# Half of the weights' low parts made by adding transfers instead of VectorE and GpSimd

## The chip, the cores and the metric

The kernel runs on one core of a Trainium2 chip. The metric is the device time of one execution in microseconds (us); the time of the kernel before is the median of three runs. The engines are named as in the profile: PE (TensorE, matrix products), PEld (its weight loads), DVE (VectorE), ACT (ScalarE), POOL (GpSimd) and SP (SyncE, which here only issues transfers). A transfer is a DMA; "SPq" is SP's own instruction stream.

## The reference

One layer of a decoder trunk on 288 positions (256 of a prompt, and 8 sequences of 4 new tokens), in float32. The width is 2048.

```
h = rmsnorm(x); proj = h @ w_in + b_in              # 2048 -> 3072: a, gate, z of 1024 each
u = a * sigmoid(gate)
c = silu(layernorm(depthwise_conv31(history + u)))  # 31 taps for each channel
d = moving_mean(history + z, windows 2, 4, 8, 16) - z
p = (d @ pool_w, per group of 256 channels) * pool_scale
x = x + concat(c, p) @ w_out                        # 2048 -> 2048
x = x + square(relu(rmsnorm(x) @ w_ff1)) @ w_ff2    # 2048 -> 8192 -> 2048
y = rmsnorm(x)
```

Outputs are y and the new histories of u and z.

## The kernel before, in words

Channels lie on the 128 partitions and the 288 positions along the free axis. Weights come from memory in blocks of 128 x 8 x 256 numbers (1 MB), one `wr` tile each, through a pool of three such tiles (`wraw`). SP issues these loads in a fixed order.

To multiply in float32 precision with products of the type float32r, each weight block is split into two parts: `hi`, the weight rounded to float32r, and `lo`, the weight minus `hi`. The function `split` does that for the two **halves** of a block (4 slices of 128 x 256, thus 128 x 1024 numbers): ACT casts the half into a `whi` tile, and another engine subtracts it from the raw weight into a `wlo` tile. `whi` and `wlo` come from pools of **four tiles each** (`wspl`), so the split of a half can start only when PE has finished the half that used the tile before. `gemm` then issues three products for every slice and each of two column blocks: hi x hi (line 250), hi x lo of the activations (line 251), lo x hi (line 252). A half is thus 24 products of 128 x 128 by 128 x 288.

Which engine subtracts is decided by a running count with the table `SHARE`: out of eight halves, so many go to POOL (in two pieces of 128 x 512), the others to DVE.

```
SHARE = {"first": 0, "second": 4, "conv": 7, "pool": 5, "pool_w": 3, "w_out": 6}
...
            turn["n"] += share
            slow = turn["n"] >= 8
            turn["n"] %= 8
```

The stages, in the order in which PE passes them:

- Input projection, 12 groups of four halves (96 products each): seven convolution groups, four pooling groups (window 16 first, then 8, 4, 2), and the last convolution group. Each group's result is a pair of PSUM banks `ac`; there are two such pairs. A convolution group is followed by its gate (`conv_pair`): a product with the row `rb` on DVE (`ag`), a sigmoid on ACT, two DVE operations into `u_all`, then 30 taps of 128 x 256 on DVE (line 340, tile `pc`) and, for the 32 sample positions, four products on POOL (line 343, `prd`). The taps have low priority and fill DVE whenever nothing else is ready. A pooling group (`pool_group`) goes DVE (`tz`), ACT (into `z_all`), POOL (line 369, one pair of sums `s` for each doubling of the window), DVE (`d`), ACT and DVE (`dx`, the hi and lo of the activations).
- `pool_w`: four small products groups of 12 on `dx`, whose weights are one block. ACT and DVE bring each result out of its banks as `px` (lines 417 and 418).
- Output projection `w_out`: 16 groups of two halves. The first eight, with the `px` activations, are split by the table; from the ninth on DVE subtracts everything.
- The two feed-forward products in four chunks, with all subtractions on DVE, and the last norm.

Every engine takes its instructions in the order in which they were put into its stream. That order comes out of the tile framework's scheduler, which runs the program with estimated durations and picks by priority; it is fixed when the kernel is built. An instruction that waits holds up everything behind it on its engine.

Halves are numbered here as in the names of the tiles: `whi9`/`wlo9` belong to the first half of the third group, 29 to 32 to the first pooling group, 45 to 48 to the last convolution group, 49 and 50 to `pool_w`, 51 to 66 to the first eight groups of the output projection.

Of the kernel before, what the change touches and what calls it, by code (L numbers as in the profile page):

```python
# [17 lines left out]
D = 2048  # L18
# [48 lines left out]

SHARE = {"first": 0, "second": 4, "conv": 7, "pool": 5, "pool_w": 3, "w_out": 6}

# [11 lines left out]
def trunk_kernel(ctx: ExitStack, tc: tile.TileContext, io):  # L81
# [43 lines left out]
    def f32(t):  # L125
        return t.bitcast(F32)
# [19 lines left out]
    def load(cuts=((0, 8),), x_cuts=()):  # L146

        raw = wraw.tile([P, 8, 256], F32, name=nm("wr"), tag="wr")
        src = io["w"][next(blocks)]
        for j, (k0, k1) in enumerate(cuts):  # L150
            if j < len(x_cuts):
                a, b = x_cuts[j]
                nc.sync.dma_start(xT[:, a:b, :], io["xT"][:, a:b, :])
            nc.sync.dma_start(raw[:, k0:k1, :], src[:, k0:k1, :])
        return raw

# [53 lines left out]

    turn = {"n": 0}

    def split(raw, share=0, cut=4):


        parts = []
        for h in range(2):
            hi = wspl.tile([P, 4, 256], F32R, name=nm("whi"), tag="whi")
            lo = wspl.tile([P, 4, 256], F32R, name=nm("wlo"), tag="wlo")
            turn["n"] += share  # L220
            slow = turn["n"] >= 8
            turn["n"] %= 8
            for k in range(0, 4, cut):
                src = raw[:, 4 * h + k : 4 * h + k + cut, :]
                nc.scalar.copy(hi[:, k : k + cut, :], src)  # L225
                eng, step = (nc.gpsimd, 2) if slow else (nc.vector, cut)
                for j in range(k, k + cut, step):
                    eng.tensor_tensor(lo[:, j : j + step, :], raw[:, 4 * h + j : 4 * h + j + step, :], hi[:, j : j + step, :].bitcast(F32), op=ALU.subtract)  # L228
            parts.append((hi, lo))
# [46 lines left out]
    def weight_groups():  # L276

        yield [split(raw0, SHARE["first"], 2), split(raw1, SHARE["first"], 2)]
        for j, (kind, _) in enumerate(SEQUENCE[1:]):
            yield [split(load(), SHARE[kind if j else "second"]) for _ in range(2)]  # L280
        getp = split(load(), SHARE["pool_w"])
        for g in GROUPS:
            yield [lambda k, m, g=g: getp(2 * g + k, m)]
        for _ in range(8):
            get = split(load(), SHARE["w_out"])
            yield [lambda k, m, get=get: get(korder[k], m)]
# [304 lines left out]
```

## Time and profile before

| | |
|---|---|
| median of three runs | 1122.64 us (1118.34 to 1123.49) |
| the profiled execution | 1121.02 us, of which its span (first to last instruction) 1119.2 us |
| PE busy | 1095.0 us, 98% of the span |
| PEld / DVE / ACT / POOL busy | 1090.7 / 646.2 / 470.1 / 185.8 us |
| mean granted TensorE clock | 0.990 |
| bytes moved | 187.0 MB, 167 GB/s |

How to read it: a group of instructions is given by line, engine, operation and tiles, with its count, its total busy time, the mean duration of one in ns, and the idle time of the engine just ahead of it with what ended that. Products are pipelined: each shows about 0.3 us, but they start some 0.13 us apart, so the number of products that start in a stretch tells more than PE's busy time. A stretch of the span gets one row with each engine's busy time and number of instructions, the granted TensorE clock, the busy share of the 16 DMA engines and the rate.

### The profile page before, as it was taken

The page shows a single profiled execution, that of the slowest core. Times are in us where ns is not written, and L with a number is a line of the kernel's source. Part 1 is how long each engine was busy: PE and PEld are TensorE (multiplying, and loading weights), DVE is VectorE, ACT ScalarE, POOL GpSimd, SP SyncE. Part 2 cuts the span into 40 slices and gives each one's busy share as a digit, 9 for nine tenths or more (in the row PEclk, how much of TensorE's full clock was granted, in tenths as well). Part 3 has the DMA queues.
Part 4 walks back from the last instruction along what each step waited for, and adds up shares of the span by engine and source line. Part 5 has one row for each costly group of instructions (what it writes and reads, how often), then busy time and mean ns, then how long its engine had stood idle before and what let it go on. Part 6 is the DMA issues. An engine that isn't in the chain of part 4 may idle for free.

```text
span 1119.2 us, 19178 instructions
## 1 busy us (share of the span) xinstructions
PE 1095.0 (98%) x8220; PEld 1090.7 (97%) x8220; DVE 646.2 (58%) x830; ACT 470.1 (42%) x578; POOL 185.8 (17%) x185
## 2 busy tenths in 40 slices
PE   9999988999999999999999999999999999999995
PEld 8999987999999999999999999999999999999995
DVE  7799999667654444444554444455444445554553
ACT  8444444465444433334443333444433334444441
POOL 1898996512100000000000000000000000000000
PEclk9999998999999999999999999999999999999997
DMA  9545456444444454544445444454544545445432
GB/s 344 186 154 185 151 132 201 154 176 161 160 168 162 161 179 153 179 159 164 175 154 182 153 168 171 155 184 152 172 167 160 180 151 177 162 159 180 152 112 85
DMA packets 31909, 187.00 MB, mean 167 GB/s; under 512 B 3408, under 2 KB 7760, under 8 KB 10448
## 3 DMA queue, kind: packets, MB, share of 16 engines
q1 hardware_dynamic: 31680, 185.73, 48.1%
q8 instruction: 64, 1.05, 0.4%
q14 instruction: 21, 0.17, 0.0%
q10 hardware_dynamic: 144, 0.05, 0.0%
HBM read 181.49 MB, written 4.28 MB: 166 GB/s over the span
## 4 chain that ended last, share of the span: by engine, by line
PE 93%; POOL 2%; DVE 2%; DMA 1%; ACT 1%; issue 1%; SPq 0%; DVEq 0%; ACTq 0%; POOLq 0%
PE ac L250 31%; PE ac L252 31%; PE ac L251 30%; POOL wlo L228 1%; POOL s L369 1%; DMA wr<-in_w 1%; PE pt L186 0%; DMA xT<-in_xT 0%; DVE xT L531 0%; ACT whi L225 0%; ACT hx L271 0%; PE pr L204 0%; DVE px L418 0%; DVE hx L272 0%; DVE pc L340 0%
## 5 line engine op out<-in xcount | busy, mean ns | idle before, releaser
L225 ACT CAST whi<-wr 128x1024 fp32r<-128x1024 f32 (+1 forms) x342 | 355.2, 1040 | 563.6 <-PE ac L251 531.9
L228 DVE TENSOR_TENSOR wlo<-wr,whi 128x1024 fp32r<-128x1024 f32 (+1 forms) x297 | 364.0, 1226 | 352.2 <-ACT whi L225 351.3
L250 PE MATMUL ac<-ax,whi 128*128 128x288 f32 x1024 | 303.4, 296 | 0.0
L250 PE MATMUL ac<-fx,whi 128*128 128x288 f32 x1024 | 303.1, 296 | 0.0
L252 PE MATMUL ac<-ax,wlo 128*128 128x288 f32 x1024 | 301.8, 295 | 0.0
L252 PE MATMUL ac<-fx,wlo 128*128 128x288 f32 x1024 | 301.8, 295 | 0.0
L251 PE MATMUL ac<-ax,whi 128*128 128x288 f32 x1024 | 298.5, 292 | 0.0
L251 PE MATMUL ac<-fx,whi 128*128 128x288 f32 x1024 | 298.5, 292 | 0.0
L251 PEld LDWEIGHTS ac<-ax,whi 128*128 128x128 f32 x1024 | 192.5, 188 | 0.1
L251 PEld LDWEIGHTS ac<-fx,whi 128*128 128x128 f32 x1024 | 192.5, 188 | 0.0
L250 PEld LDWEIGHTS ac<-ax,whi 128*128 128x128 f32 x1024 | 192.4, 188 | 0.1
L250 PEld LDWEIGHTS ac<-fx,whi 128*128 128x128 f32 x1024 | 192.4, 188 | 0.0
L252 PEld LDWEIGHTS ac<-ax,wlo 128*128 128x128 f32 x1024 | 191.5, 187 | 0.0
L252 PEld LDWEIGHTS ac<-fx,wlo 128*128 128x128 f32 x1024 | 191.5, 187 | 0.0
L228 POOL TENSOR_TENSOR wlo<-wr,whi 128x512 fp32r<-128x512 f32 x90 | 119.4, 1358 | 48.1 <-ACT whi L225 48.1
L252 PE MATMUL ac<-hx,wlo 128*128 128x288 f32 x384 | 114.8, 299 | 1.5 <-DVE wlo L228 1.3
L250 PE MATMUL ac<-hx,whi 128*128 128x288 f32 x384 | 114.8, 299 | 0.3 <-ACT whi L225 0.3
L251 PE MATMUL ac<-hx,whi 128*128 128x288 f32 x384 | 112.7, 294 | 0.0
L340 DVE SCALAR_TENSOR_TENSOR pc<-u_all,vec,pc 128x256 f32<-128x256 f32 x232 | 99.4, 480 | 1.2
L252 PEld LDWEIGHTS ac<-hx,wlo 128*128 128x128 f32 x384 | 72.6, 189 | 3.4 <-DVE wlo L228 2.5
L250 PEld LDWEIGHTS ac<-hx,whi 128*128 128x128 f32 x384 | 72.9, 190 | 0.6 <-ACT whi L225 0.5
L251 PEld LDWEIGHTS ac<-hx,whi 128*128 128x128 f32 x384 | 72.9, 190 | 0.1
(109 smaller groups left out, 828.4 us busy)
## 6 DMA issues: line engine op xcount, KB each, us to landing
wr<-in_w SPq DMA_DIRECT2D x167, 1024.0 KB, 4.9
xT<-in_xT SPq DMA_DIRECT2D x8, 288.0 KB, 5.7
wr<-in_w SPq DMA_DIRECT2D x8, 256.0 KB, 5.6
out_u_out<-u_all SPq DMA_DIRECT2D x1, 1208.0 KB, 8.9
out_yT<-xT SPq DMA_DIRECT2D x2, 576.0 KB, 2.9
u_all<-in_hist_c SPq DMA_DIRECT2D x8, 136.0 KB, 6.1
out_z_out<-z_all SPq DMA_DIRECT2D x1, 668.0 KB, 8.1
z_all<-in_hist_p SPq DMA_DIRECT2D x4, 152.0 KB, 5.6
```

The costliest lines, as they stand in the source:

```text
L225: nc.scalar.copy(hi[:, k : k + cut, :], src)
L228: eng.tensor_tensor(lo[:, j : j + step, :], raw[:, 4 * h + j : 4 * h + j + step, :], hi[:, j : j + step, :].bitcast(F32), op=ALU.subtract)
L250: nc.tensor.matmul(b, wh, xh, start=k == 0, stop=False)
L251: nc.tensor.matmul(b, wh, xl, start=False, stop=False)
L252: nc.tensor.matmul(b, wl, xh, start=False, stop=k == n - 1)
L340: nc.vector.scalar_tensor_tensor(out=dst, in0=up[:, w : w + SEQ], scalar=cwv[:, w : w + 1], in1=pc, op0=ALU.mult, op1=ALU.add)
L369: nc.gpsimd.tensor_tensor(s2[:, m, 2 * w - 1 :], s[:, m, 2 * w - 1 :], s[:, m, w - 1 : ZL - w], op=ALU.add)
```

## The change

The table of shares is replaced by a table of ways for each half of a group: "V" subtracts on DVE, "G" on POOL, and "D" is new. For a D half ACT first casts the weight into `hi` as before, then writes -`hi` into the `lo` tile, and then POOL issues a transfer that fetches the same half of the weight block a second time from memory and adds it to what is in the `lo` tile (`accum_op=ALU.add`). `load` returns the source beside the tile for that. With the first D half three small DVE operations take the difference between the subtraction and the transfer's result for one slice and add it, times 2^20, to the activations' last tile, so a difference would be seen in the output.

```diff
-SHARE = {"first": 0, "second": 4, "conv": 7, "pool": 5, "pool_w": 3, "w_out": 6}
+WAYS = {"first": ("VV", "VV"), "second": ("VG", "VG"), "conv": ("DG", "DG"), "pool": ("DG", "DV"), "pool_w": ("DV",), "w_out": ("DG",)}
...
-        return raw
+        return raw, src
...
-    def split(raw, share=0, cut=4):
+    def split(raw, ways="VV", cut=4):
+        raw, src = raw
         parts = []
-        for h in range(2):
+        for h, way in enumerate(ways):
             hi = wspl.tile([P, 4, 256], F32R, name=nm("whi"), tag="whi")
             lo = wspl.tile([P, 4, 256], F32R, name=nm("wlo"), tag="wlo")
-            turn["n"] += share
-            slow = turn["n"] >= 8
-            turn["n"] %= 8
             for k in range(0, 4, cut):
...
+                if way == "D":
+                    continue
+                eng, step = (nc.gpsimd, 2) if way == "G" else (nc.vector, cut)
...
+            if way == "D":
+                nc.scalar.activation(lo, f32(hi), AF.Copy, scale=-1.0)
+                if not proof:
+                    proof.append(tmp("q")[:, 0:256])
+                    nc.vector.tensor_tensor(proof[0], raw[:, 4 * h, :], f32(hi[:, 0, :]), op=ALU.subtract)
+                nc.gpsimd.dma_start(lo, src[:, 4 * h : 4 * h + 4, :], accum_op=ALU.add)
...
-            yield [split(load(), SHARE[kind if j else "second"]) for _ in range(2)]
-        getp = split(load(), SHARE["pool_w"])
+            yield [split(load(), ways) for ways in WAYS[kind if j else "second"]]
+        getp = split(load(), *WAYS["pool_w"])
```

Of the 62 halves from the second group to the eighth group of the output projection, POOL subtracted 45 and DVE 17; now POOL subtracts 26, DVE 7, and 29 are D halves. The feed-forward products are split as before.

The scheduler's order moves with it. First, ACT in a convolution group (the casts of halves 17 to 20; `ag` is the gate of the group before). Before:

```order
L225 CAST whi17_857<-wr9_855 128x1024
L225 CAST whi18_861<-wr9_855 128x1024
L225 CAST whi19_868<-wr10_866 128x1024
L225 CAST whi20_873<-wr10_866 128x1024
L326 ACTIVATE ag4_878<-ag4_878,vec_85 128x288
```

Now:

```order
L226 CAST whi17_862<-wr9_860 128x1024
L233 ACTIVATE wlo17_863<-whi17_862 128x1024
L226 CAST whi18_867<-wr9_860 128x1024
L226 CAST whi19_874<-wr10_872 128x1024
L233 ACTIVATE wlo19_875<-whi19_874 128x1024
L226 CAST whi20_879<-wr10_872 128x1024
L339 ACTIVATE ag4_884<-ag4_884,vec_85 128x288
```

Two negations of 128 x 1024 have come in per group, each right behind its cast.

Second, POOL from the end of the convolution groups into the first pooling group (`prd` are a convolution group's sample products, `s` the pooling sums, `sum_c` a sum over convolution results). Before:

```order
L343 TENSOR_TENSOR prd7_1417<-u_all_87,vec_85 128x8x31 x4
L228 TENSOR_TENSOR wlo34_1529<-wr17_1522,whi34_1528 128x512 x2
L349 TENSOR_TENSOR sum_c_213<-c1_506,c2_717 128x288
L228 TENSOR_TENSOR wlo36_1540<-wr18_1533,whi36_1539 128x512 x2
L369 TENSOR_TENSOR s1_1550<-z_all_88 128x422 x2
L228 TENSOR_TENSOR wlo37_1673<-wr19_1670,whi37_1672 128x512 x2
L369 TENSOR_TENSOR s2_1553<-s1_1550 128x420 x2
L228 TENSOR_TENSOR wlo39_1684<-wr20_1681,whi39_1683 128x512 x2
L369 TENSOR_TENSOR s3_1556<-s2_1553 128x416 x2
L228 TENSOR_TENSOR wlo40_1689<-wr20_1681,whi40_1688 128x512 x2
L369 TENSOR_TENSOR s4_1559<-s3_1556 128x408 x2
```

Now:

```order
L356 TENSOR_TENSOR prd7_1424<-u_all_87,vec_85 128x8x31 x4
L237 DMA wlo33_1532<-in_w 128x1024
L231 TENSOR_TENSOR wlo34_1537<-wr17_1529,whi34_1536 128x512 x2
L237 DMA wlo35_1544<-in_w 128x1024
L382 TENSOR_TENSOR s1_1558<-z_all_88 128x422 x2
L382 TENSOR_TENSOR s2_1561<-s1_1558 128x420 x2
L237 DMA wlo37_1681<-in_w 128x1024
L382 TENSOR_TENSOR s3_1564<-s2_1561 128x416 x2
L231 TENSOR_TENSOR wlo38_1686<-wr19_1678,whi38_1685 128x512 x2
L382 TENSOR_TENSOR s4_1567<-s3_1564 128x408 x2
L237 DMA wlo39_1693<-in_w 128x1024
```

The issues of the adding transfers stand in POOL's stream among the sums and the subtractions, each behind what is written above it.

Third, ACT around `pool_w` (the sigmoid `ag8` and the table load belong to the last convolution group; `px1` to `px4` bring out the four results). Before:

```order
L417 ACTIVATE px1_2171<-ac13_2158,vec_85 128x288 x2
L225 CAST whi52_2232<-wr26_2225 128x1024
L326 ACTIVATE ag8_2109<-ag8_2109,vec_85 128x288
L384 CAST dx4_1998<-d4_1991 128x2x288
L168 ACT_TABLE_LOAD
L168 ACTIVATE few_111<-ag8_2109 128x1
L225 CAST whi53_2370<-wr27_2368 128x1024
L417 ACTIVATE px2_2189<-ac14_2176,vec_85 128x288
L337 ACTIVATE pc8_2115<-u_all_87,vec_85 128x256
L417 ACTIVATE px3_2207<-ac15_2194,vec_85 128x288
L417 ACTIVATE px2_2189<-ac14_2176,vec_85 128x288
```

Now:

```order
L339 ACTIVATE ag8_2119<-ag8_2119,vec_85 128x288
L168 ACT_TABLE_LOAD
L168 ACTIVATE few_111<-ag8_2119 128x1
L430 ACTIVATE px1_2181<-ac13_2168,vec_85 128x288
L350 ACTIVATE pc8_2125<-u_all_87,vec_85 128x256
L430 ACTIVATE px1_2181<-ac13_2168,vec_85 128x288
L226 CAST whi53_2380<-wr27_2378 128x1024
L430 ACTIVATE px2_2199<-ac14_2186,vec_85 128x288
L233 ACTIVATE wlo53_2381<-whi53_2380 128x1024
L430 ACTIVATE px2_2199<-ac14_2186,vec_85 128x288
L430 ACTIVATE px3_2217<-ac15_2204,vec_85 128x288
```

All `px` now stand behind the sigmoid and the table load: on PE the first `pool_w` products (those that make `px1`) used to stand inside the last convolution group, 22 products ahead of its end, and now all four groups of them follow it.

More of the change, by code (lines that the diff above doesn't have):

```diff
@@ L276, in weight_groups @@
     def weight_groups():
[L278 removed]
+        yield [split(raw, ways, 2) for raw, ways in zip((raw0, raw1), WAYS["first"])]
         for j, (kind, _) in enumerate(SEQUENCE[1:]):
[L280 to L281 removed]
+            yield [split(load(), ways) for ways in WAYS[kind if j else "second"]]
+        getp = split(load(), *WAYS["pool_w"])
         for g in GROUPS:
@@ L284, in weight_groups @@
         for _ in range(8):
-            get = split(load(), SHARE["w_out"])
+            get = split(load(), *WAYS["w_out"])
             yield [lambda k, m, get=get: get(korder[k], m)]
```

12 lines of the change are left out of this document (7 added, 5 removed).

## The prediction

> **What bounds the kernel now.** I read the page's head first: PE is busy 98% of the span, so the change can win only what PE loses now, and can lose wherever it makes PE wait. The table by stretches of the span shows where PE loses; the count behind PE's busy time is of products begun.
>
> ```profile
> span 1119.2 us, 19178 instructions
> PE 1095.0 (98%) x8220; PEld 1090.7 (97%) x8220; DVE 646.2 (58%) x830; ACT 470.1 (42%) x578; POOL 185.8 (17%) x185
> ...
> core 0: us, PE busy (x) PEld busy (x) DVE busy (x) ACT busy (x) POOL busy (x), PEclk, DMA share, GB/s
> ...
> 140.00:154.00 14.00, 14.00 (x108) 14.00 (x107) 13.96 (x28) 5.56 (x10) 14.00 (x14) 1.00 0.44 152
> 154.00:168.00 14.00, 10.09 (x66) 9.29 (x65) 13.65 (x23) 5.79 (x9) 14.00 (x11) 0.92 0.58 116
> 168.00:182.00 14.00, 9.11 (x51) 8.66 (x50) 13.02 (x30) 9.36 (x15) 10.12 (x10) 0.83 0.64 223
> 182.00:196.00 14.00, 13.66 (x90) 13.56 (x91) 12.81 (x26) 4.73 (x8) 7.16 (x7) 0.88 0.64 175
> 196.00:210.00 14.00, 14.00 (x107) 13.89 (x106) 7.71 (x14) 5.18 (x6) 9.20 (x9) 1.00 0.46 153
> ...
> 400.00:700.00 300.00, 300.00 (x2271) 300.00 (x2270) 140.25 (x127) 109.87 (x111) 0.00 (x0) 1.00 0.48 165
> ```
>
> A full stretch of 14 us holds 107 or 108 products (300 us hold 2271, so one per 0.132 us). From 154 to 196 us there are 66 + 51 + 90 = 207 instead of some 322: 115 x 0.132 = 15.2 us lost, of which PE is idle for 3.91 + 4.89 + 0.34 = 9.1 us; most of the rest is the clock (0.92, 0.83, 0.88). These are the end of the input projection and `pool_w`. Taking off about 0.7 us that the products for the mean need there, **14.5 us** can be won; before and after it, in the stages that the change touches, PE waits for nothing. The waits themselves, by time:
>
> ```profile
> start us, us, engine line op out<-in xcount [idle before <-releaser]
> ...
> 166.42 0.61 PE L252 MATMUL ac<-dx,wlo 128*128 128x288 f32 x1 [3.75 <-DVE wlo L228]
> 166.83 0.44 PE L250 MATMUL ac<-dx,whi 128*128 128x288 f32 x1
> 167.07 0.44 PE L251 MATMUL ac<-dx,whi 128*128 128x288 f32 x1
> ...
> 174.96 0.40 PE L250 MATMUL ac<-dx,whi 128*128 128x288 f32 x1 [1.26 <-DVE px L418]
> ...
> 182.34 0.40 PE L250 MATMUL ac<-dx,whi 128*128 128x288 f32 x1 [3.97 <-DVE px L418]
> ```
>
> One wait is for a `lo` part that DVE made late, two for banks (`px`). After the first, products start 0.24 us apart (166.83, 167.07): an idle stretch of this length costs clock as well. In the stretch ahead DVE (13.96 of 14) and POOL (14.00) are both full: subtractions, taps and pooling sums are late together.
>
> **The change part by part.** The prices of what is moved:
>
> ```profile
> L228 DVE TENSOR_TENSOR wlo<-wr,whi 128x1024 fp32r<-128x1024 f32 x289 | 358.6, 1241 | 351.8 <-ACT whi L225 350.9
> L225 ACT CAST whi<-wr 128x1024 fp32r<-128x1024 f32 x334 | 350.5, 1050 | 563.3 <-PE ac L251 531.9 <-PE ac L252 14.2 <-DMA wr<-in_w 9.7
> ...
> L228 POOL TENSOR_TENSOR wlo<-wr,whi 128x512 fp32r<-128x512 f32 x90 | 119.4, 1358 | 48.1 <-ACT whi L225 48.1
> ...
> L343 POOL TENSOR_TENSOR prd<-u_all,vec 128x248 f32<-128x248 f32 x32 | 24.5, 800 | 3.6 <-DVE u_all L330 2.6 <-POOL wlo L228 0.6 <-DVE c L345 0.3
> ...
> L369 POOL TENSOR_TENSOR s<-z_all 128x422 f32<-128x422 f32 x8 | 8.9, 1140 | 0.0
> L369 POOL TENSOR_TENSOR s<-s 128x420 f32<-128x420 f32 x6 | 8.1, 1374 | 0.0
> ```
>
> DVE loses 10 halves, 10 x 1.24 = 12.4 us; POOL loses 19 halves of two pieces, 38 x 1.36 = 51.6 us, and gets 29 issues; ACT gets 29 negations of the cast's size, 29 x 1.05 = 30.5 us, in stretches where it is busy under 6 of 14 us, so on their own they lie beside other work. The three small DVE operations on the first D half are under 2 us once, among taps of low priority, and cost nothing unless the transfer is late there by more than the gate work ahead of them.
>
> *The gain.* The 3.75 us wait for DVE's `lo` should go: the taps' backlog is smaller, and half 50 now stands on DVE behind the pooling work and no longer among taps. The waits for `px` should not go. All four `pool_w` groups now follow the last convolution group, and ACT brings out `px1` only after the gate and the table load:
>
> ```profile
> L168 ACT ACT_TABLE_LOAD x4 | 5.1, 1283 | 1.2 <-PEq L573 1.2
> L418 DVE SCALAR_TENSOR_TENSOR px<-ac,vec,px 128x288 fp32r<-128x288 f32 x8 | 4.1, 511 | 0.1
> ...
> L417 ACT ACTIVATE px<-ac,vec 128x288 fp32r<-128x288 f32 x8 | 3.9, 496 | 4.5 <-DVE px L418 4.5
> ...
> L325 DVE TENSOR_TENSOR ag<-ac,rb 128x576 f32<-128x576 f32 x8 | 6.0, 749 | 6.0 <-ACT rb L395 5.6 <-PE ac L252 0.4
> ```
>
> Counted from the end of the last convolution group: gate on DVE 0.75, sigmoid and table load to about 2.8, `px1` with the start of a tap row between its halves to 4.4, DVE 4.9. The third `pool_w` group, which needs those banks, could start at 3.8 (two groups of 12 x 0.132 and a product for the mean) and starts at 4.9. By the same walk down ACT (cast 53, `px2`, negation 53, `px2`) the fourth starts at 8.0 instead of 6.5, and the first `w_out` group, which needs `px3` behind cast 54, at 12.2 instead of 9.6. That is 1.1 + 1.5 + 2.6 = 5.2 us idle, and for some of it the clock, say 2 us. Of 14.5 us remain about 7, so I take a **gain of 7 us**; the bounds are 0 (another wait takes the place) and 14.5.
>
> *The loss.* Four `whi` and four `wlo` tiles serve in turn. In the undisturbed part ACT shows the turn:
>
> ```profile
> 399.86 1.05 ACT L225 CAST whi<-wr 128x1024 fp32r<-128x1024 f32 x1 [2.12 <-PE ac L251]
> 403.04 1.05 ACT L225 CAST whi<-wr 128x1024 fp32r<-128x1024 f32 x1 [2.12 <-PE ac L251]
> ```
>
> A half lasts 3.17 us, and each cast waits for PE to give back a tile. So from the moment a tile comes back there are 3 x 3.17 = 9.5 us until PE needs it filled. A DVE half takes 1.05 + 1.24 of these. A D half takes the cast, the negation (2.1 us together), the wait w for POOL to reach the issue, and X from issue to landing: PE waits where **w + X exceeds 7.4 us**. As the tiles go round in fours, every four halves pay the larger excess of their two D halves. The wait w comes from POOL's order. In a convolution group, on a clock that starts when the first tile comes back: issue at 2.1, subtraction 4.2 to 7.0, issue 8.4, subtraction 10.6 to 13.3, `prd` to 16.5, while the next first issue is ready at 12.7 + 2.1 = 14.8: w about 1.6, so X over 5.8 costs, in five groups. In the first pooling group the sums wait for ACT's `z_all` until about 2.8 after the group begins; two pairs (2.3 + 2.7) take POOL to 7.8, the issue of 37, one pair more, subtraction 38 and the last pair to about 15.5, where issue 39 has been ready since 11.6: w about 3.9, X over 3.5 costs. For the next group's worst I get w 1.7, for the third 0.5. In `w_out` POOL has only issues and subtractions, w is 0, over four turns.
>
> X stands in no row. The nearest rows:
>
> ```profile
> wr<-in_w SPq DMA_DIRECT2D x167, 1024.0 KB, 4.9
> ...
> out_yT<-xT SPq DMA_DIRECT2D x2, 576.0 KB, 2.9
> ...
> L154 SPq DMA_DIRECT2D wr<-in_w x175: 327/328/704, 1.2 to 1074.9; - x175
> ...
> DMA to landing us min/median/max: 4.4/4.9/9.9
> ```
>
> Below: a plain 576 KB in 2.9 us plus an issue like SP's, 0.3: 3.2. Above: the slowest landing of a block, 9.9; nothing excludes more. Between: in the long stretch a share of 0.48 moves 165 GB/s, so the full engines do 344 GB/s, a 1 MB block keeps them 3.05 us, and 1.85 of its 4.9 us is fixed. An add reads 512 KB of weights and 512 KB of the tile; if the engines do these one after the other, that is 3.05 + 1.85 + about 0.5 for the issue = 5.4 alone. But one such transfer per two halves (6.35 us) is another 0.48 of the engines beside the loads' 0.48: 0.96 in all, so the two will overlap. Sharing 0.48 of the time adds 1.5, queueing at 0.96 something more. I take **X = 7.5**, midway between 5.4 and 9.9.
>
> With X = 7.5: convolution 5 x 1.7 = 8.5; pooling 4.0 + 1.8 + 0.6 = 6.4; `w_out` 4 x 0.1 = 0.4. Loss 15, gain 7: 8 us slower. The profiled execution (1121.0: span 1119.2 and 1.8 around it) would become 1129; it lies 1.6 below the median 1122.6, so against medians **1131 us**. At other X the same sum gives a loss of 0 (3.2), 2 (5), 3 (6), 11 (7), 21 (8) and 43 (9.9).
>
> Two rules of the Trainium skill pull apart here. "Collectives: The Full Stack", section "The bandwidth ceiling: the fold count and why AG ≠ RS ≠ AR", has a reduce slower than a copy because "the add needs **two source reads**" on one ring; by it the 3.05 us above is right. It speaks against the change; no run here shows it yet. "DMA: Bandwidth & Descriptors", section "Anatomy of one DMA — SWDGE (gpsimd) path", fits about 2.0 us plus bytes at 436 GB/s for a transfer issued on GpSimd; by that, an estimate of X is 3.2 us for 512 KB and the change wins its whole gain.
>
> **The rivals.**
> *Faster.* The tile's read costs no engine time of its own and X is under 5.3, as the 576 KB row suggests (the page's fit, named above, says the same). For it: the loads leave half of the engines free. Against: the add must fetch the old values. The loss is then at most 2 us, the gain 7, up to 12 if POOL's and DVE's relief shortens the `px` waits as well: 1122.6 - 5 to - 11, **1115 us**.
> *No change.* X is 5.5 to 6.9: late only behind the pooling sums, 3 to 9 us, against 7 won: 1118 to 1127, **1121 us**. For it: 5.4 alone, and the loads have three tiles of room to step aside.
> *Much slower.* With 0.96 of the engines asked for, the transfers set the pace, and beside the outputs `out_z_out` and `out_u_out` around 160 to 185 us (share 0.58 and 0.64 already) there is no room. X stays at 9.9 or beyond: 43 - 7, **1159 us**, and 14 us more for each further us of X.
> *It does not add.* If the transfer only copied, X would be that of the faster rival, and the time too; nothing in the profile speaks for that, and I give it no share of its own.
>
> **How the numbers follow.** The forecast (X from 7 to 9, its own range 1126 to 1146) gets 0.32, much slower 0.18, no change 0.26, faster 0.24. What can be told from no change is 0.5%, 5.6 us: slower is 0.32 + 0.18 = 0.50, same 0.26, faster 0.24. The range leaves out about a tenth on each side: from 1111, the faster rival with nearly all of its gain, to 1160, the much slower one at its lower end.
>
> **What would show it.** Right: PE waits in the convolution groups, from 45 to 130 us, each before a line-265 product, for a `wlo` whose transfer landed about 7 to 9 us after issue, some 1.7 us per group; the longest behind the first pooling group's sums; a DMA share near 0.9; DVE and POOL no longer full; the `px` waits still there after the last convolution group. Wrong: no such waits, because transfers land within 5 us; or waits on every D half, with landings over 10 us; or a gain at `pool_w` of over 10 us, which would mean that the `px` walk above is not what holds PE there.

## The result: slower by 0.6%, and the profile after

| | before | after |
|---|---|---|
| median of ten runs | 1122.66 us (1118.34 to 1123.87) | 1130.41 us (1125.60 to 1132.88) |
| ratio of the medians | | 1.0063, 95% interval 1.0047 to 1.0080 |
| profiled execution, span | 1121.02 us, 1119.2 us | 1127.32 us, 1125.5 us |
| mean granted TensorE clock | 0.990 | 0.986 |

The change makes the kernel 0.5 to 0.8% slower. The forecast was 1131 us. In the code of after, lines 263, 264 and 265 are the products that were 250, 251 and 252 before, line 231 is the subtraction, 233 the negation, 237 the issue of the adding transfer, and 431 writes `px`.

First the head of the page, its DMA queues and its DMA issues (the last number is the median from issue to landing):

```profile
span 1125.5 us, 19210 instructions
PE 1092.7 (97%) x8220; PEld 1087.4 (97%) x8220; DVE 639.3 (57%) x823; ACT 499.4 (44%) x607; POOL 154.0 (14%) x176
...
q1 hardware_dynamic: 31680, 185.73, 47.9%
q0 software_dynamic: 4176, 15.21, 7.7%
...
wr<-in_w SPq DMA_DIRECT2D x167, 1024.0 KB, 4.9
wlo<-in_w POOLq DMA_DIRECT2D x29, 512.0 KB, 6.0
```

ACT got 29 us, as costed. DVE lost 6.9 us and not 12.4, POOL 31.8 and not 51.6: each of the 29 issues keeps POOL busy for 0.87 us (median), which had no price in the prediction. The adding transfers are the queue q0: 15.21 MB kept 7.7% of 16 engines' span busy, 86.7 us of all engines or 2.99 us for each of the 29, against 3.05 us worked out for two streams of 512 KB. They landed 6.0 us after the issue in the median, not 7.5. Next what PE waited for, in sum (us in total, number of waits, the longest):

```profile
PE ac L265 <- DMA wlo<-in_w: 11.9, 5, 5.6
PE ac L263 <- DVE px L431: 5.3, 3, 2.8
...
PE ac L265 <- DVE wlo L231: 1.3, 5, 0.4
```

DVE's `lo` no longer counts (1.3 us in five waits of 0.4 at most), `px` waits as before, and 11.9 us have come in for transfers. Here is where each wait lies:

```profile
43.82 0.61 PE L265 MATMUL ac<-hx,wlo 128*128 128x288 f32 x1 [5.58 <-DMA wlo<-in_w]
44.23 0.44 PE L263 MATMUL ac<-hx,whi 128*128 128x288 f32 x1
44.47 0.44 PE L264 MATMUL ac<-hx,whi 128*128 128x288 f32 x1
...
149.53 0.40 PE L265 MATMUL ac<-hx,wlo 128*128 128x288 f32 x1 [1.23 <-DMA wlo<-in_w]
163.73 0.40 PE L265 MATMUL ac<-hx,wlo 128*128 128x288 f32 x1 [1.24 <-DMA wlo<-in_w]
173.91 0.40 PE L265 MATMUL ac<-hx,wlo 128*128 128x288 f32 x1 [3.62 <-DMA wlo<-in_w]
187.44 0.40 PE L263 MATMUL ac<-dx,whi 128*128 128x288 f32 x1 [2.03 <-DVE px L431]
190.13 0.61 PE L263 MATMUL ac<-dx,whi 128*128 128x288 f32 x1 [0.46 <-DVE px L431]
195.65 0.61 PE L263 MATMUL ac<-px,whi 128*128 128x288 f32 x1 [2.77 <-DVE px L431]
```

One long wait stands at the first adding transfer of all (half 9), one in the fourth pooling group, two in the last convolution group, none over 0.2 us in the fourth to seventh convolution groups, from 58 to 110 us. After the long one, products start 0.24 us apart: the clock is halved. Short stretches show for how long (begin and end, length, then busy time and number of instructions of PE, PEld, DVE, ACT and POOL, the granted clock, the DMA share and GB/s):

```profile
42.00:44.00 2.00, 0.18 (x1) 0.18 (x2) 2.00 (x6) 0.57 (x1) 2.00 (x4) 0.50 0.99 188
44.00:46.00 2.00, 2.00 (x9) 2.00 (x10) 2.00 (x5) 0.00 (x0) 2.00 (x3) 0.50 1.06 287
46.00:48.00 2.00, 2.00 (x10) 2.00 (x10) 2.00 (x5) 0.00 (x0) 1.53 (x3) 0.50 0.88 369
48.00:49.00 1.00, 1.00 (x7) 1.00 (x6) 1.00 (x2) 0.10 (x1) 0.00 (x0) 0.61 0.04 16
```

The granted clock is 0.50 to past 48 us, so of the 4.9 us behind the wait about half is lost as well: a wait of 5.6 us costs some 8.

### The profile page after: what moved, and what is told of

The parts are those of the page before. It is cut to its first block, busy times and chain, and to the rows that moved or that the text cites. A ratio compares the mean times of both kernels' runs of the same rounds, so it can differ in the third digit from the quotient of the medians.

```text
span 1125.5 us, 19210 instructions
## 1 busy us (share of the span) xinstructions
PE 1092.7 (97%) x8220; PEld 1087.4 (97%) x8220; DVE 639.3 (57%) x823; ACT 499.4 (44%) x607; POOL 154.0 (14%) x176
## 3 DMA queue, kind: packets, MB, share of 16 engines
q0 software_dynamic: 4176, 15.21, 7.7%
q8 instruction: 64, 1.05, 0.4%
## 4 chain that ended last, share of the span: by engine, by line
PE 91%; DVE 3%; DMA 3%; issue 1%; ACT 1%; POOL 1%; SPq 0%; DVEq 0%; POOLq 0%; ACTq 0%
PE ac L263 31%; PE ac L264 30%; PE ac L265 30%; DMA wlo<-in_w 2%; DVE pc L353 1%; DMA xT<-in_xT 1%; PE pt L186 0%; POOL wlo L231 0%; DVE dx L398 0%; DVE xT L544 0%; DVE wlo L231 0%; ACT whi L226 0%; ACT hx L284 0%; DVE px L431 0%; DVE u_all L343 0%
## 5 line engine op out<-in xcount | busy, mean ns | idle before, releaser
L231 DVE TENSOR_TENSOR wlo<-wr,whi 128x1024 fp32r<-128x1024 f32 (+1 forms) x287 | 349.0, 1216 | 347.1 <-ACT whi L226 346.0
L265 PE MATMUL ac<-ax,wlo 128*128 128x288 f32 x1024 | 298.6, 292 | 0.0
L265 PE MATMUL ac<-fx,wlo 128*128 128x288 f32 x1024 | 298.4, 291 | 0.0
L265 PE MATMUL ac<-hx,wlo 128*128 128x288 f32 x384 | 115.9, 303 | 13.2 <-DMA wlo<-in_w 11.9
L231 POOL TENSOR_TENSOR wlo<-wr,whi 128x512 fp32r<-128x512 f32 x52 | 70.6, 1396 | 41.3 <-ACT whi L226 41.1
```

The source lines that it names most:

```text
L265: nc.tensor.matmul(b, wl, xh, start=False, stop=k == n - 1)
```

## The experiments

The kernels are the changed one with the edit shown, unless it says otherwise.

**What a transfer costs.** Two kernels keep the split's orders but change the transfer. `e5_no_transfer` leaves it out, so that a D half multiplies by -hi in place of the low part; `e3_plain_copy` copies the weight over -hi instead of adding it.

```diff
-                nc.gpsimd.dma_start(lo, src[:, 4 * h : 4 * h + 4, :], accum_op=ALU.add)
```

> The changed kernel without the 29 adding transfers: lo stays -hi, so the second weight part is left out of the result (and the three small DVE operations act on that). Casts, negations and the division over DVE and POOL stay. Theory A and B alike: the 11.9 us that PE waits for transfers go, with 3 to 4 us of clock, so a profiled span near 1110 instead of 1125.5, while the waits for px (5.3 us) stay. Rival C (the 30 us of negations on ACT, or the new order, are the price): the span stays above 1119.

```diff
-                nc.gpsimd.dma_start(lo, src[:, 4 * h : 4 * h + 4, :], accum_op=ALU.add)
+                nc.gpsimd.dma_start(lo, src[:, 4 * h : 4 * h + 4, :])
```

> The same 29 transfers as plain copies: they overwrite -hi with the weight instead of adding, so lo is the whole weight and the result is not the reference's. If an add reads two streams one after the other, a copy keeps the engines half as long (about 1.5 us instead of 3.0 for 512 KB: 15.2 MB in 3.9% of the 16 engines' span instead of 7.7%) and lands in about 4.5 us instead of 6.0. If adding is free, both stay: 6.0 us and 7.7%.

Without transfers: 1115.84 us. With plain copies: 1121.54 us, and this in the queues and issues of that kernel:

```profile
q0 software_dynamic: 4176, 15.21, 4.3%
...
wlo<-in_w POOLq DMA_DIRECT2D x29, 512.0 KB, 4.9
```

The same bytes take 4.3% of the engines (1.66 us a transfer) instead of 7.7% (2.99), and land in 4.9 us instead of 6.0. So the add costs the engines nearly a second stream of the same size, as the reading of the tile would, and a plain copy is not cheap either: 4.9 us for 512 KB, as much as for a block of 1 MB. The span without transfers is 1114.0 us, not near 1110; the 1110 was counted down from 1125.5, a profile in which the products stand closer together (next paragraphs).

**The same kernels again.** The profiled execution of after (1127.32 us) lies well below its median. Two more profiles of it and one more of before were taken.

> The changed kernel once more, for a second profile. Two questions. (a) From 400 to 700 us the kernel before begins 2271 products and the changed kernel 2290, by the same code. If that is a state of the single execution, this profile may show either number; if it belongs to the kernel, it shows 2290 again and the one of the kernel before 2271 again. (b) If the wait of 5.6 us for the first transfer of the third group comes from POOL's fixed order (a subtraction ahead of the issue), it is here again within 0.5 us, and from 28 to 56 us about 60 products are missing again. If it was chance of the start loads, it differs by more. The 5.3 us operation on DVE at 144 us should be gone or elsewhere if it was chance; then 140 to 168 us lose little.

> The kernel before once more, for a second profile, as the other half of the question on the spacing of products: 2271 products from 400 to 700 us if it belongs to the kernel, 2271 or 2290 if to the execution. From 154 to 196 us about 207 products again if the waits at the end of the input projection come from the fixed orders.

> The changed kernel a third time, for a third profile. The first had a median landing of 6.0 us and no wait in the fourth to seventh convolution groups, with 2290 products from 400 to 700 us; the second 7.5 us, waits of 0.3 to 1.0 us in those groups, and 2272 products. If landing and spacing are two independent accidents of an execution, they may come in any pairing; if they go together, 6.0 comes with 2290 and 7.5 with 2272 again. The wait at the third group is 5.6 us in any case, and the px waits sum to about 5.

After came out at 1134.22 and 1130.60 us, before at 1120.72 us. The rows of two stretches, first of before and then of the three profiles of after in order, with the products begun in brackets behind PE:

```profile
70.00:140.00 70.00, 70.00 (x531) 70.00 (x530) 69.93 (x145) 29.19 (x41) 66.28 (x59) 1.00 0.47 165
400.00:700.00 300.00, 300.00 (x2271) 300.00 (x2270) 140.25 (x127) 109.87 (x111) 0.00 (x0) 1.00 0.48 165
```

```profile
70.00:140.00 70.00, 70.00 (x532) 70.00 (x531) 68.17 (x148) 42.79 (x56) 52.67 (x56) 1.00 0.93 247
400.00:700.00 300.00, 300.00 (x2290) 300.00 (x2289) 141.87 (x129) 111.66 (x114) 0.00 (x0) 1.00 0.48 166
```

```profile
70.00:140.00 70.00, 66.95 (x498) 65.56 (x497) 64.86 (x143) 38.79 (x48) 49.94 (x53) 1.00 0.89 232
400.00:700.00 300.00, 300.00 (x2272) 300.00 (x2271) 140.57 (x128) 111.27 (x113) 0.00 (x0) 1.00 0.48 166
```

```profile
70.00:140.00 70.00, 70.00 (x532) 70.00 (x531) 68.14 (x147) 42.78 (x56) 52.66 (x56) 1.00 0.92 246
400.00:700.00 300.00, 300.00 (x2271) 300.00 (x2271) 140.93 (x128) 111.14 (x113) 0.00 (x0) 1.00 0.48 167
```

Two things differ between executions of one kernel. From 400 to 700 us, where no transfer adds anything, 2290 or 2271 products begin, a spacing of 0.1310 or 0.1321 us at a granted clock of 1.00. Over the 6144 feed-forward products that is 6.7 us. It belongs to the execution: after shows 2290, 2272 and 2271, before 2271 twice. And the transfers landed in 6.0, 7.5 and 6.1 us in the median; at 7.5 they cost the sixth and seventh convolution groups and the pooling groups, too (498 products instead of 531 from 70 to 140 us), while the long wait at half 9 came every time (5.58, 5.73 and 5.62 us). Landing and spacing do not go together: 6.1 us came with 2271 products.

With that, kernels of the same spacing can be set side by side, by products begun. The counts are those of the stretches named (`after`, 2nd and 3rd are its later profiles):

| us | before | no transfer | plain copy | after, 2nd | after, 3rd |
|---|---|---|---|---|---|
| 28 to 70 | 318 | 318 | 276 | 252 | 257 |
| 70 to 140 | 531 | 532 | 535 | 498 | 532 |
| 140 to 154 | 108 | 108 | 102 | 96 | 97 |
| 154 to 196 | 206 | 242 | 244 | 240 | 210 |
| 196 to 252 | 432 | 432 | 433 | 403 | 427 |
| 252 to 300 | 365 | 369 | 368 | 368 | 368 |
| sum, against before | 1960 | +41 | -2 | -103 | -69 |
| times 0.132 us | | 5.4 faster | 0.3 slower | 13.6 slower | 9.1 slower |
| span against 1119.2 | | 5.2 faster | 0.6 slower | 13.2 slower | 9.6 slower |

The sums agree with the spans within 0.6 us, so nothing is lost elsewhere. Taking work off DVE and POOL wins 5 us, nearly all of it from 154 to 196 us; the transfers cost 14.8 us in the third profile and 18.4 in the second; as plain copies they cost 5.8. The first profile of after has the other spacing: brought to the spacing of the others by the 6.7 us, its span of 1125.5 becomes 1132.2, 13.0 us slower than before, and its transfers cost 18.2 us. So at equal spacing the three profiles are 9.6 to 13.2 us slower than before, and the medians only 7.8. Which spacing the executions without a profile had is not on record; the medians may mix the two.

**The first transfers.** In `e1_third_as_second` the third group is split like the second, without transfers. In `e7_third_dv` DVE takes the G halves of the third group, so that no subtraction of POOL stands ahead of the first issues.

```diff
-            yield [split(load(), ways) for ways in WAYS[kind if j else "second"]]
+            yield [split(load(), ways) for ways in WAYS[kind if j > 1 else "second"]]
```

> The third group is split like the second (VG, VG), so the first two adding transfers (halves 9 and 11) are gone and 27 remain. Theory A (the price lies where the change begins: the transfer of half 9 is issued at 34.7 us, behind a POOL subtraction and among the loads of the start, lands 9.1 us later and costs 5.6 us of waiting and some 3 us of half clock): about 8 us less than the changed kernel, 1122. Rival B (every turn of four tiles with adding transfers pays a little, as the prediction had it): only about 1.5 us less, 1129.

```diff
-            yield [split(load(), ways) for ways in WAYS[kind if j else "second"]]
+            yield [split(load(), ways) for ways in (("DV", "DV") if j == 1 else WAYS[kind if j else "second"])]
```

> The changed kernel, with DVE in place of POOL for the second halves of the third group, so that no subtraction of POOL stands ahead of the first issues. Theory (POOL's order and the crowded start loads add up): the issue of half 9 comes about 1.6 us earlier, at 33.1, it still takes some 9 us to land among the start loads, and the wait of 5.6 us shrinks to about 4; the whole kernel is 2 to 3 us faster than the changed one, 1127 to 1128. Rival 1 (the start loads alone are the cause): the transfer lands when the loads let it, the wait stays 5.6 and the time 1130. Rival 2 (POOL's order alone): the landing falls to about 6 as well, the wait is under 1 us and the time is that of the kernel whose third group has no transfers, about 1120.

`e1_third_as_second` took 1120.10 us (1117.68 to 1127.43, ten runs), ratio to before 1.0000, interval 0.9980 to 1.0019. So without the third group's two transfers the loss against before is gone: what the 27 others cost and what the relief wins are about equal in the medians. Its profiled execution, 1125.62 us, is one of its slowest (its transfers took 7.5 us in the median from 70 to 126 us, with three more waits of 0.6 to 2.6 us there and just behind), and there the first transfers wait again, one group later, by 2.17 us. POOL shows why:

```profile
42.73 4.74 POOL L356 TENSOR_TENSOR prd<-u_all,vec 128x248 f32<-128x248 f32 x7
47.41 1.00 POOL L237 DMA_DIRECT2D wlo<-in_w  x1
48.17 2.83 POOL L231 TENSOR_TENSOR wlo<-wr,whi 128x512 fp32r<-128x512 f32 x2
```

Its negation ended at 43.2 us, and the issue came at 47.4, behind seven sample products that the fixed order puts ahead of it. It landed after 5.6 us. The second transfer of that group, issued 3.3 us behind the first and beside two weight loads, took 10.6.

`e7_third_dv` took 1130.95 us (1128.54 to 1132.32), ratio 1.0079, interval 1.0064 to 1.0093. The issue of half 9 moved from 34.73 to 33.4 us, the landing after it stayed at 9.0 us, and the wait fell from 5.58 to 4.27:

```profile
42.45 0.61 PE L265 MATMUL ac<-hx,wlo 128*128 128x288 f32 x1 [4.27 <-DMA wlo<-in_w]
83.41 0.40 PE L265 MATMUL ac<-hx,wlo 128*128 128x288 f32 x1 [0.83 <-DMA wlo<-in_w]
135.02 0.40 PE L265 MATMUL ac<-hx,wlo 128*128 128x288 f32 x1 [0.50 <-DMA wlo<-in_w]
```

So 1.3 us of the wait came from POOL's order, as the theory had it. The rest was not due to loads of the start: the last of the histories had landed by 30.2 us in after and by 29.5 here, before the issue. The rows of issues and landings show another crowd. In after the transfers of halves 9 and 11 go out at 34.73 and 36.67 and a weight load at 34.80, and the DMA share is 0.98 or more from 38 to 44 us; three such pieces of 2.99, 3.05 and 2.99 us are 9.0 us of all engines, and half 9's took 9.05. Here the three stand at 33.37, 36.60 and 33.38. In the kernel with three tiles below, the second transfer is 11.8 us behind the first, and the first took 7.1 us; PE waits 2.74 us for it, although the ring is a tile smaller. That the crowd alone makes up the rest was not tested. The 2 to 3 us that the kernel should have won in all did not come, and why is open: its one profile has transfers of 6.5 us in the median and further waits in the sixth convolution group (0.83) and the third pooling group (0.50).

**The room in the ring.** Three `whi` and three `wlo` tiles in place of four, in the changed kernel and, as a control, in the kernel before.

```diff
-    wspl = ctx.enter_context(tc.tile_pool(name="wspl", bufs=4))
+    wspl = ctx.enter_context(tc.tile_pool(name="wspl", bufs=3))
```

> The changed kernel with three whi and three wlo tiles in turn in place of four. Theory (the room in the ring decides, 9.5 us with four tiles, 2 x 3.17 = 6.3 with three, less 2.1 for cast and negation): a D half with w near 0 and a landing of 6.0 is late by 6.0 - 4.2 = 1.8 us, one with 7.5 by 3.3; in the steady convolution groups from 70 to 126 us (eight D halves) PE waits for transfers in nearly every one, 10 to 25 us in all, against none or 2.8 in the two profiles with four tiles. Over 29 transfers this makes some 50 to 100 us, less what one wait gives to the next half: 1160 to 1220 us. Rival (the transfers run well ahead and only single late ones count): the waits grow by under 1 us per half, and the time stays under 1150.

> The control for the kernel with three tiles: the kernel before, with three whi and three wlo tiles. A half split by DVE takes 1.05 + 1.24 = 2.3 us of 6.3, one split by POOL 1.05 + 2.7 = 3.8 plus its place behind sample products and sums. Theory: outside the end of the input projection little changes in the steady convolution groups (under 5 us of waits from 70 to 126), pooling and the end of the input projection lose more than before; 1121 to 1140 us, well below the changed kernel with three tiles. Rival (three tiles are too few for any way of splitting): over 1150.

The changed kernel took 1150.06 us, the one before 1126.27; both executions have 2290 products from 400 to 700 us. What PE waited for from 70 to 126 us in the changed kernel, and then in the control:

```profile
PE ac L265 <- DMA wlo<-in_w: 7.3, 4, 2.0
```

```profile
PE ac L252 <- DVE wlo L228: 1.1, 1, 1.1
PE ac L252 <- POOL wlo L228: 0.2, 1, 0.2
```

Each wait has about the expected size: 7.3/4 = 1.8 us, where a landing of 5.7 and a room of 4.2 make 1.5. There is one for every group (the fifth to seventh convolution groups and the first pooling group) and not for every D half: after a wait the second D half of the group comes in time. So the total expected by the theory, 1160 to 1220, was too high, and the time lies just above the rival's 1150. With a tile less the change lies 23.8 us behind before, instead of 9.6 to 13.2 at equal spacing with four. So the room decides.

**Fewer transfers.** If the middle groups are free, a kernel with transfers there alone could beat both. `e6_conv4to7` has them in the convolution groups from the fourth on, the last one included (ten transfers, not the eight of its expectation); `e10_middle` in the fourth to seventh, with DVE instead of POOL for one half of the fourth; `e11_a` in the fifth to seventh, with the `pool_w` block split by POOL. The other halves go to DVE and POOL.

```diff
-WAYS = {"first": ("VV", "VV"), "second": ("VG", "VG"), "conv": ("DG", "DG"), "pool": ("DG", "DV"), "pool_w": ("DV",), "w_out": ("DG",)}
+WAYS = {"first": ("VV", "VV"), "second": ("VG", "VG"), "conv": ("DG", "DG"), "pool": ("GV", "GV"), "pool_w": ("VV",), "w_out": ("VG",)}
...
+            yield [split(load(), ways) for ways in WAYS[kind if j > 1 else "second"]]
```

> Adding transfers only in the fourth to seventh convolution groups (8 of them); the third group like the second, the pooling groups, pool_w and the output projection subtract on DVE and POOL again (half and half). Theory A: these eight are free, since PE waits nowhere from 70 to 140 us in the changed kernel, and they relieve DVE and POOL ahead of the pooling groups: 1122 or less, down to 1115 if that relief shortens the wait at pool_w. Rival B (each turn of four halves with two transfers pays about 1.7 us): 4 turns, above 1126.

```diff
+WAYS = {"first": ("VV", "VV"), "second": ("VG", "VG"), "conv": ("DG", "DG"), "pool": ("DG", "DV"), "pool_w": ("VV",), "w_out": ("VG",)}
+GROUP_WAYS = (("VG", "VG"), ("VG", "VG"), ("DV", "DG"), ("DG", "DG"), ("DG", "DG"), ("DG", "DG"), ("GV", "GV"), ("GV", "GV"), ("GV", "GV"), ("GV", "GV"), ("VG", "GV"))
...
+            yield [split(load(), ways) for ways in GROUP_WAYS[j]]
```

> Transfers only where the trace of the changed kernel showed no cost: the first halves of the fourth to seventh convolution groups, 8 transfers, and in the fourth with DVE instead of POOL for half 14, so that no subtraction of POOL lies ahead of the first issue. The third and the last convolution group, pooling, pool weights and output projection are split by DVE and POOL alone. Theory (a transfer costs nothing if POOL issues it within 1.4 us of the negation and outputs do not crowd it): no wait for a transfer longer than 1 us, 28 to 140 us full but for the fourth group's first (4.2 us behind POOL in the kernel with transfers in all convolution groups but the third; here eight sample products, some 5.5 us, less what is already done, are still ahead of it, so up to 1 us), and 1116 to 1119 us, 0.2 to 0.6% faster than before. Rival (the taps' backlog on DVE decides at the end of the input projection, whatever is done ahead of it): waits there as before, some 9 us, and 1121.

```diff
+WAYS = {"first": ("VV", "VV"), "second": ("VG", "VG"), "conv": ("DG", "DG"), "pool": ("DG", "DV"), "pool_w": ("GG",), "w_out": ("VG",)}
+GROUP_WAYS = (('VG', 'VG'), ('VG', 'VG'), ('VG', 'VG'), ('DG', 'DG'), ('DG', 'DG'), ('DG', 'DG'), ('GV', 'GV'), ('GV', 'GV'), ('GV', 'GV'), ('GV', 'GV'), ('VG', 'VG'))
```

> Transfers in the fifth to seventh convolution groups alone (6 of them), where the first issue has only four sample products ahead of it on POOL; the weights of the pool stage are split by POOL alone, so that no subtraction of that block stands on DVE among the taps (that wait was 3.75 us before, and 2.95 us in the kernel with transfers in the fourth to seventh groups alone); the other halves as DVE and POOL share them. Theory: no wait for a transfer over 1 us, no wait for DVE's lo over 1 us at the pool weights; the waits for px and the gate, 5 to 7 us, stay; 1115 to 1119 us, 0.2 to 0.6% faster than before. Rival (DVE's backlog of taps moves the wait to the next thing on DVE, the gate ag or px): the waits from 154 to 196 us sum to 8 us or more, and 1120 to 1123.

| | median us | ratio to before | interval |
|---|---|---|---|
| `e6_conv4to7` | 1119.78 | 0.9987 | 0.9976 to 0.9997 |
| `e10_middle` | 1119.79 | 0.9998 | 0.9981 to 1.0014 |
| `e11_a` | 1122.32 | 1.0004 | 0.9991 to 1.0017 |

At best 0.1%, not the 0.2 to 0.6% of the last two theories. The waits at the end of `e11_a` say why; they sum to 10.0 us, against 9.0 in before (lines 264, 266 and 432 here are 263, 265 and 431 of after):

```profile
173.33 0.61 PE L266 MATMUL ac<-dx,wlo 128*128 128x288 f32 x1 [5.00 <-POOL wlo L232]
182.83 0.61 PE L264 MATMUL ac<-dx,whi 128*128 128x288 f32 x1 [4.35 <-DVE px L432]
189.12 0.40 PE L264 MATMUL ac<-px,whi 128*128 128x288 f32 x1 [0.68 <-DVE px L432]
```

Moving the `pool_w` block from DVE to POOL moved the wait from DVE to POOL. The profiled execution of `e10_middle`, 1126.94 us, one of two among its twelve runs that lie above 1121, has there 2.95 us for DVE's `lo`, 3.02 for the gate and 3.79 for `px`. Transfers in the middle take nothing from the end, where the kernel loses; the rival of these two runs was right. Nor were the middle groups free: PE waits for transfers 2.16 us in the profile of `e6_conv4to7` and 2.39 in that of `e10_middle`, both at half 13, the first D half, and 1.88 in that of `e11_a` at half 21, where the two theories allowed 1 us at most. In the first two the issue of half 13 stood 4.2 us behind its negation on POOL; `e10_middle`, which took a subtraction of POOL away from there, did not shorten that.

## Why the prediction was right, and where not

**What bounds the kernel, and the prize.** Right. Nearly all that `e5_no_transfer` won lies from 154 to 196 us, where 14.5 us were seen to be lost (14.0 by the prediction's own 0.132 us, by which 42 us hold 318 products and not 322).

**The gain, forecast 7 us.** The subtractions' relief measured alone was 5.2 us of span. The 3.75 us wait for DVE's `lo` went, and the `px` walk down ACT came out in the sum: forecast 1.1 + 1.5 + 2.6 = 5.2 us idle, measured 2.03 + 0.46 + 2.77 = 5.26, the first two terms each off by 1 us and in opposite directions. The clock's share was set too low: without transfers 318 - 242 = 76 products or 10.0 us are still missing from 154 to 196 us, of which PE is idle for 42 - 36.1 = 5.9 and the products for the mean take 0.7; the other 3.4 are the clock (granted 0.92 over these 42 us), where 2 were allowed.

**The loss, forecast 15 us at X = 7.5.** Measured as after minus `e5_no_transfer` at equal spacing: 18.2, 18.4 and 14.8 us in the three profiles, each one execution against one. The sum came near, its terms less so:

- *X.* The parts were right (2.99 us of engine time against 3.05; the shortest landing in the three profiles of after is 5.4, 5.4 and 5.5, near the 5.4 worked out for a transfer alone, although the 0.5 us for the issue in that sum stood in no row; on POOL an issue takes 0.87), the surcharge for sharing too large for two executions, 6.0 and 6.1, and right for the one with 7.5. At X = 6 the prediction's formula gives a loss of 3 us (3.8 when its terms are added again). At 6.0 and 6.1 it measured 18.2 and 14.8.
- *Convolution groups, 5 x 1.7 = 8.5.* The step that failed: the groups were taken as equal, each with a landing of 7.5. The third cost 5.6 us of waiting, the fourth to seventh nothing (2.0 us in the profile with X = 7.5). The limit of 7.4 on w + X itself holds: in the first profile the first D halves of the fifth to seventh groups have w of 1.34, 0.93 and 1.27 and landings of 5.58, 5.37 and 5.89, sums of 6.3 to 7.2 and no wait; half 41 has 1.57 + 7.28 = 8.85 and waits 1.23. At half 9 two things came on top. The first stands ahead of the issue, on ACT and POOL:

```profile
29.33 1.05 ACT L226 CAST whi<-wr 128x1024 fp32r<-128x1024 f32 x1 [2.11 <-DMA wr<-in_w]
31.10 1.06 ACT L226 CAST whi<-wr 128x1024 fp32r<-128x1024 f32 x1 [0.72 <-PE ac L264]
32.05 1.06 ACT L233 ACTIVATE wlo<-whi 128x1024 fp32r<-128x1024 f32 x1
```

```profile
32.23 2.54 POOL L231 TENSOR_TENSOR wlo<-wr,whi 128x512 fp32r<-128x512 f32 x2 [2.10 <-ACT whi L226]
34.73 0.99 POOL L237 DMA_DIRECT2D wlo<-in_w  x1
36.67 0.86 POOL L237 DMA_DIRECT2D wlo<-in_w  x1 [0.95 <-PE pr L204]
```

  The cast at 29.33 is half 9's; it waited for its weight block. The next, at 31.10, is half 10's (POOL's subtraction of half 10 starts right behind it); it waits until PE gives back half 6's tile at 31.01. Half 9's negation stands behind both and starts at 32.05, 4.2 us after half 5's tile came back (27.84) and not 1.05 us. PE needs half 9's low part at 38.24, 10.4 us after 27.84, so the room was there; the order on ACT took 3.2 us of it. (The block's lateness is not what counts: in the second profile the block landed 0.7 us earlier, and the negation started at 31.96 all the same.) The issue then came at 34.73 (w 1.6, as forecast). The second thing is the landing, 9.05 us later at 43.78, beside the transfer of half 11 and a weight load. PE went on at 43.82, 5.58 us after 38.24.
- *Pooling, 6.4, with 4.0 behind the first group's sums.* The first group's sums cost nothing: the issue of half 39 came 0.9 us after its negation and not 3.9, as POOL, with fewer subtractions, was done with the sums (the stretch to 140 us is full). In the first profile 1.23 us came in the fourth pooling group, which had no price, and 1.24 + 3.62 us in the last convolution group, which the prediction had left out of its five. In this last group w + X is 7.1 and 6.8, under the limit; the lateness arose ahead of the negation. The chain there is one of engines that stand in order. DVE's `dx` took 5.33 us where the other three took 0.75 to 0.97:

```profile
144.20 5.33 DVE L398 TENSOR_TENSOR dx<-d,dx 128x576 fp32r<-128x576 f32 x1
```

```profile
153.24 0.51 ACT L376 ACTIVATE z_all<-tz,vec 128x256 f32<-128x256 f32 x1 [3.99 <-DVE tz L373]
...
164.34 0.67 ACT L397 CAST dx<-d 128x576 fp32r<-128x576 f32 x1 [4.58 <-DVE d L395]
164.92 1.05 ACT L226 CAST whi<-wr 128x1024 fp32r<-128x1024 f32 x1
166.00 1.06 ACT L233 ACTIVATE wlo<-whi 128x1024 fp32r<-128x1024 f32 x1
```

  `tz` is late (152.46), ACT stands before it, the pooling sums and `d` are late, ACT stands again, and the cast and negation of half 47 behind it; its issue at 167.36 landed 6.5 us later, and PE waited 3.62. That each step waits for the one before is in the rows; that a `dx` of 1 us would have saved the 3.62 was not tried. It is not the only way to such a wait: in `e6_conv4to7` no `dx` took over 1.6 us, and the same two halves waited 2.11 and 2.52 us, the second with a landing of 9.1.
- *The clock.* The loss side had no term for it. The 5.6 us wait alone took another 2.5. From 196 to 252 us 24, 29 and 5 products are missing in the three profiles (432 against 408, 403 and 427), but these are mostly no further cost: they lie right behind the last `px` wait (12 of the 24 from 196 to 200 us, at a clock of 0.63), which the kernel without transfers has too, only ahead of 196 us. About 10 of the 24 go from 222.9 to 226.3 us, at a clock of 0.50 with no wait of PE, behind 24 small products (128x96 by 128x1). Neither the other two profiles of after nor before show that; the cause is open.

**The rivals.** *Faster* fell with X: the tile's read costs engine time (7.7 against 4.3%). *No change* had the landing right, 5.5 to 6.9, in two of three profiles, but put the waits behind the pooling sums, and only 3 to 9 us of them. *Much slower* needs landings of 9.9; in the first profile only the third group's two transfers (9.1 and 10.2 us) and two beside the outputs (12.9 and 12.4) come near or pass it. So the number came out right although its main term, equal waits in the convolution groups, did not: a loss near the right sum stood at other places. That is luck in part, and so is the last digit: the medians differ by 7.8 us, the forecast's 8, but the profiles at equal spacing by 9.6 to 13.2.

**What was said to show it.** A DMA share near 0.9 (0.89 to 0.93 from 70 to 140 us), POOL not full (52.7 of 70 us), `px` still waiting: seen. DVE was hardly less full, 68.2 us against 69.9. The longest wait stood at half 9 and not behind the first pooling group's sums. Waits of 1.7 us in each convolution group from 45 to 130 us: not seen at four tiles, and seen with 1.8 us at three.

On the two rules of the Trainium skill weighed in the prediction the runs decide. "Collectives: The Full Stack", section "The bandwidth ceiling: the fold count and why AG ≠ RS ≠ AR", has a reduce read two sources; the trace agrees (2.99 us of engines for an add against 1.66 for a copy). "DMA: Bandwidth & Descriptors", section "Anatomy of one DMA — SWDGE (gpsimd) path", gives by its fit 3.2 us for 512 KB; a plain copy took 4.9 here beside the loads and an add 6.0 to 7.5, so the fit is too low for this traffic.

## What to carry to other kernels

A transfer that stands in for engine work has to be timed at its first use and at stage borders, not only in the steady state. There the ring of buffers hid it; at its first use the engines' order brought its issue out late, a second transfer and a load went out within 2 us of it, and the halved clock behind the long wait added nearly half of it again. Ask first whether the engine that is relieved holds PE anywhere; here it did so in one place only, and of the 9.0 us of waits at the end of the input projection 5.9 (`px`, the gate) stayed even without any transfer. And compare a kernel's profiles with one another before reading a difference of half a per cent out of two single executions.

## What was not expected of the hardware

*Two spacings of the same products.* In all fourteen profiles of this study 400 to 700 us hold 2271 or 2272 products, or 2290, never anything between, at a granted clock of 1.00 and with no wait. Before showed 2271 twice, after both values, before with three tiles 2290. On two of the three numbered chips of the record both values came as well (with different kernels), so neither the kernel nor the chip alone decides it. It is worth 6.7 us here; what draws it was not found.

*The landing of an adding transfer differs between executions as well.* The same code gave medians of 6.0, 7.5 and 6.1 us. From 70 to 140 us, where engines and orders are alike, it was 5.9, 7.6 and 5.8, and the weight loads beside them took 5.3, 7.1 and 5.2: the traffic as a whole went slower in the second. The cause is open.

*A DVE operation held for 5.3 us.* The `dx` of the first pooling group took 5.33, 5.34 and 5.35 us in the three profiles of after, and each time POOL ran without a gap from just before it:

```profile
143.67 2.82 POOL L231 TENSOR_TENSOR wlo<-wr,whi 128x512 fp32r<-128x512 f32 x2
146.19 1.05 POOL L362 TENSOR_TENSOR sum_c<-sum_c,c 128x288 f32<-128x288 f32 x1
146.95 1.95 POOL L382 TENSOR_TENSOR s<-s 128x416 f32<-128x416 f32 x2
148.61 1.12 POOL L237 DMA_DIRECT2D wlo<-in_w  x1
```

"SBUF — State Buffer", section "🔬 SBUF: two separate sides", of the Trainium skill says that DVE and GpSimd share a pair of ports, held for a whole instruction by whichever starts first when a DVE operation has two inputs there and the GpSimd operation reads there. The rows fit this, and go further: the `dx` ended at 149.53, 0.6 us behind the last of five POOL operations in a row (143.67 to 148.90), not behind one. In `e7_third_dv` it was another operation, a `d` of only 128x30 numbers: it took 6.22 us, from 141.23, while POOL ran six operations without a gap from 141.21 to 147.38. In before, in two stretches with POOL busy 14 of 14 us, `dx` took 1.04 and 0.95 us, so it is not the rule.
